# Batched matmul: stores of batches 28 to 30 through SP's queue, x loaded four batches ahead, transposes beside their own matmuls

## The chip, the cores and the metric

One core of a Trainium2 chip; the experiments ran on three chips, each time beside the kernel before. The metric is device time in microseconds (us). Where the text gives a moment ("at 496.45 us"), it is counted from the start of the profiled span, which is shorter than the device time of the same run. A landing is the issue of a transfer plus its time to landing; the views print the latter to 0.1 us, the hundredths are from the trace itself. One run was profiled for each kernel, so a moment comes from one run and a time from several.

## The reference

```python
def setup_inputs():
    batch, m, k, n = 32, 512, 1024, 768
    return {"x": randn(batch, m, k) as float32, "weight": randn(batch, k, n) as float32}

def reference(x, weight):
    return np.matmul(x, weight).astype(np.float32)
```

In float32 a batch is 2.10 MB of x, 3.15 MB of weight ("w" below) and 1.57 MB of output. All 32 batches are 167.77 MB read and 50.33 MB written, and nothing can be reused between batches.

## The kernel before

Loads go through GpSimd's queue (the "software queue") and are converted to bf16 on the way. x is transposed by TensorE against an identity matrix; the products are gathered in PSUM, copied to SBUF and stored. Batches 28 to 31 load w in pieces (`CHUNKED`), so that matmuls can begin on the first piece.

```python
    CHUNKED = {B - 4: (4, 4), B - 3: (4, 4), B - 2: (4, 4), B - 1: (4, 2, 2)}
    AHEAD = 3
    # ... w_pool bufs=4, x_pool bufs=4, xT_pool bufs=8, out_pool bufs=7 ...

    def load_x(b):      # GpSimd's queue, float32 in HBM -> bf16 in SBUF
        xs[b] = x_pool.tile([P, MT, K], BF16, name="x_sb")
        nc.gpsimd.dma_start(out=xs[b], in_=x_view[b])
    # ... load_w: the same, in the pieces of CHUNKED ...

        for b in range(1, AHEAD):
            load_x(b)
            load_w(b)
        ready = {}
        for b in range(B):
            if b + AHEAD < B:
                load_x(b + AHEAD)
                load_w(b + AHEAD)
            if b > 0:
                nc.gpsimd.dma_start(out=out_view[b - 1], in_=outs[b - 1])
            outs[b] = out_pool.tile([P, MT * N], F32, name="out_sb")
            # ... batches not in CHUNKED: transposes and matmuls, then `continue` ...
            xT = ready.pop(b, None) or {mt: transpose(b, mt) for mt in range(MT)}
            # ...
            for n in CHUNKED[b]:
                last = at + n == KT
                for mt in range(MT):
                    if last and b + 1 < B:      # the NEXT batch's transposes
                        ready.setdefault(b + 1, {})[mt] = transpose(b + 1, mt)
                    matmuls(pms[mt // 2], mt % 2, xT[mt], b, range(at, at + n), True)
                    # ... evacuate; the last batch is stored in two halves on SP's queue ...
```

Each engine has a program of its own. In PE's program of the last four batches, the last matmuls of a batch stand behind the transposes of the next one, which need the next x. The timeline below shows that they do wait there.

Of the kernel before, what the change touches and what calls it, by code (L numbers as in the profile page):

```python
# [1 line left out]

# [5 lines left out]

F32 = mybir.dt.float32
BF16 = mybir.dt.bfloat16  # L10


@with_exitstack
def kernel(
    ctx: ExitStack,
    tc: tile.TileContext,
    x: bass.AP,
    weight: bass.AP,
    out: bass.AP,
):  # L20
    nc = tc.nc
    B, M, K = x.shape
    _, _, N = weight.shape
    P = 128
    MT = M // P
    KT = K // P
    JT = KT // 2
    N2 = 2 * N
    CHUNKED = {B - 4: (4, 4), B - 3: (4, 4), B - 2: (4, 4), B - 1: (4, 2, 2)}
    AHEAD = 3  # L30

    const = ctx.enter_context(tc.tile_pool(name="const", bufs=1))
    first_pool = ctx.enter_context(tc.tile_pool(name="first", bufs=1))
    w_pool = ctx.enter_context(tc.tile_pool(name="w", bufs=4))
    x_pool = ctx.enter_context(tc.tile_pool(name="x", bufs=4))
    xT_pool = ctx.enter_context(tc.tile_pool(name="xT", bufs=8))
    out_pool = ctx.enter_context(tc.tile_pool(name="out", bufs=7))
    tpsum = ctx.enter_context(tc.tile_pool(name="tpsum", bufs=2, space=bass.MemoryType.PSUM))
    mpsum = ctx.enter_context(tc.tile_pool(name="mpsum", bufs=2, space=bass.MemoryType.PSUM))



    w_view = weight.rearrange("b (ki ko) n -> b ki ko n", ki=P)
    x_view = x.rearrange("b (mi mo) k -> b mi mo k", mi=P)
    out_view = out.rearrange("b (mi mo) n -> b mi (mo n)", mi=P)

    xs, ws, outs = {}, {}, {}

    def banks():
        return [mpsum.tile([P, 512], F32, name=f"pm{i}") for i in range(3)]  # L50

    def load_x(b):
        xs[b] = x_pool.tile([P, MT, K], BF16, name="x_sb")
        nc.gpsimd.dma_start(out=xs[b], in_=x_view[b])  # L54

    def load_w(b):
        ws[b] = w_pool.tile([P, KT, N], BF16, name="w_sb")
        at = 0
        for n in CHUNKED.get(b, (KT,)):
            nc.gpsimd.dma_start(out=ws[b][:, at:at + n, :], in_=w_view[b, :, at:at + n, :])  # L60
            at += n

    def transpose(b, mt):

        pt = tpsum.tile([P, JT, P], F32, name="pt")
        pairs = xs[b].bitcast(F32)
        for j in range(JT):
            nc.tensor.transpose(pt[:, j, :], pairs[:, mt, j::JT], ident)  # L68
        xT = xT_pool.tile([P, JT, P, 2], BF16, name="xT")
        nc.vector.tensor_copy(  # L70
            xT.rearrange("p j m r -> p (j m r)"), pt.bitcast(BF16).rearrange("p j m -> p (j m)")
        )
        return xT

    def transpose_first(mt):

        xT = xT_pool.tile([P, JT, P, 2], BF16, name="xT")
        for h in range(2):
            pt = tpsum.tile([P, JT, P], F32, name="pt")
            for i in range(JT):  # L80
                nc.tensor.transpose(pt[:, i, :], x_first[:, mt, JT * h + i::KT], ident)  # L81
            nc.vector.tensor_copy(  # L82
                xT[:, 2 * h:2 * h + 2].rearrange("p j m r -> p j r m"),
                pt.rearrange("p (j r) m -> p j r m", r=2),
            )
        return xT



    SPLITS = (  # L90
        ((0, 0, 0, 512), (1, 0, 512, N - 512)),
        ((1, N - 512, 0, 1024 - N), (2, 0, 1024 - N, N2 - 1024)),
    )

    def matmuls(pm, half, xT, b, kos, together):
        for ko in kos:
            for i, (bank, at, off, size) in enumerate(SPLITS[half]):
                shares = half == 1 and i == 0
                nc.tensor.matmul(  # L99
                    pm[bank][:, at:at + size],  # L100
                    xT[:, ko // 2, :, ko % 2],
                    ws[b][:, ko, off:off + size],
                    start=(ko == 0 and not (together and shares)),
                    stop=(ko == KT - 1),
                    skip_group_check=together,
                )

    def evacuate(b, pair, pm):
        o = outs[b][:, pair * N2:(pair + 1) * N2]
        nc.scalar.copy(o[:, 0:512], pm[0])  # L110
        nc.vector.tensor_copy(o[:, 512:1024], pm[1])  # L111
        nc.scalar.copy(o[:, 1024:N2], pm[2])  # L112

    with tc.manual_schedule():
        x_first = first_pool.tile([P, MT, K], F32)
        nc.sync.dma_start(x_first, x_view[0])
        load_w(0)
        ident = const.tile([P, P], F32)
        make_identity(nc, ident)
        for b in range(1, AHEAD):  # L120
            load_x(b)
            load_w(b)

        ready = {}
        for b in range(B):
            if b + AHEAD < B:
                load_x(b + AHEAD)
                load_w(b + AHEAD)
            if b > 0:
                nc.gpsimd.dma_start(out=out_view[b - 1], in_=outs[b - 1])  # L130
            outs[b] = out_pool.tile([P, MT * N], F32, name="out_sb")
            if b not in CHUNKED:
                turn = transpose if b else lambda _, mt: transpose_first(mt)
                xT = {mt: turn(b, mt) for mt in (0, 1)}
                for pair in range(2):
                    pm = banks()
                    for half in range(2):
                        if pair == 0:
                            matmuls(pm, half, xT[half], b, range(KT), False)
                            xT[2 + half] = turn(b, 2 + half)  # L140
                        else:
                            matmuls(pm, half, xT[2 + half], b, range(KT), False)
                    evacuate(b, pair, pm)
                continue
            xT = ready.pop(b, None) or {mt: transpose(b, mt) for mt in range(MT)}
            pms = [banks() for _ in range(2)]
            at = 0
            for n in CHUNKED[b]:
                last = at + n == KT
                for mt in range(MT):  # L150
                    if last and b + 1 < B:
                        ready.setdefault(b + 1, {})[mt] = transpose(b + 1, mt)
                    matmuls(pms[mt // 2], mt % 2, xT[mt], b, range(at, at + n), True)
                    if last and mt % 2 == 1:
                        pair = mt // 2
                        evacuate(b, pair, pms[pair])
                        if b == B - 1:
                            cols = slice(pair * N2, (pair + 1) * N2)
                            nc.sync.dma_start(out_view[b, :, cols], outs[b][:, cols])
                at += n  # L160


# [1 line left out]
_INS = ['x', 'weight']  # L164
_OUTS = [((32, 512, 768), 'float32')]


# [23 lines left out]
```

## Time and profile before

| | before |
|---|---|
| device time, median of the first 3 runs | 516.96 us (516.54 to 517.15) |
| profiled span | 516.0 us |
| software queue's packets, share of 16 engines' span | 98.9% |
| TensorE (PE) busy | 83% |
| last piece of w lands | 496.45 us |
| last matmul ends | 508.5 us |
| last store lands | 514.8 us |

These are lines of the page of the kernel before. The DMA row gives the busy share of the 16 DMA engines in tenths, in 40 slices of the span (9 means 90% or more); the queue lines give packets, bytes on the SBUF side, and the share of 16 engines' time.

```profile
span 516.0 us, 5924 instructions
PE 426.4 (83%) x2528; PEld 279.6 (54%) x2576; DVE 129.7 (25%) x196; ACT 76.3 (15%) x129; POOL 53.4 (10%) x105
...
DMA  8999999999999999999999999999999999999996
...
q0 software_dynamic: 14256, 131.60, 98.9%
q1 hardware_dynamic: 432, 3.67, 1.9%
...
HBM read 167.77 MB, written 50.33 MB: 423 GB/s over the span
...
DMA 88%; PE 9%; issue 1%; DVE 0%; ACT 0%; POOLq 0%
```

The DMA engines are busy for 90% or more of each slice from the second to the last but one.

The tail needs a closer look. This is the timeline of PE before: start, duration, instruction, count, and in brackets how long PE had been idle and what ended that.

```profile
479.18 6.66 PE L99 MATMUL pm<-w_sb,xT 128*128 128x256 bf16 x39
489.12 0.75 PE L68 MATMUL pt<-ident,x_sb 128*128 128x128 f32 x4 [3.28 <-DMA x_sb<-in_x_dram]
```

Line 68 is the transpose of batch 31. PE idled 3.28 us for x of batch 31 while batch 30's last matmuls stood behind it, although the last w of batch 30 had landed at 480.55. This is the wait that the change aims at.

Now the same tail by stretches of time. The last two numbers of a line are the share of the DMA engines that was busy and GB/s.

```profile
core 0: us, PE busy (x) PEld busy (x) DVE busy (x) ACT busy (x) POOL busy (x), PEclk, DMA share, GB/s
496.00:506.00 10.00, 9.95 (x64) 6.16 (x63) 1.38 (x2) 1.17 (x2) 0.53 (x1) 1.00 0.99 420
506.00:509.00 3.00, 2.54 (x16) 1.36 (x14) 1.33 (x2) 2.14 (x4) 0.00 (x0) 1.00 0.50 211
509.00:511.00 2.00, 0.00 (x0) 0.00 (x0) 0.05 (x1) 0.16 (x1) 0.00 (x0) 1.00 1.01 415
511.00:513.00 2.00, 0.00 (x0) 0.00 (x0) 0.00 (x0) 0.00 (x0) 0.00 (x0) 1.00 0.80 326
```

From 506 to 509 us half of the engines' time is unused, and yet the stores go on landing about 3.66 us apart (503.80, 507.45, 511.11). We read this as: each transfer is spread over the engines and has landed when the slowest part is through; some engines have run empty by then, others never do. The records carry no engine number, so this reading is inferred.

These are the last piece of w (issued at 468.65) and the last store (issued at 509.18); the last number is the time from issue to landing:

```profile
w_sb<-in_weight_dram POOLq DMA_DIRECT2D x1, 384.0 KB, 27.8
out_dram<-out_sb SPq DMA_DIRECT2D x1, 768.0 KB, 5.6
```

### The profile page before, as it was taken

How to read it: one execution, taken by the hardware profiler on the slowest of the kernel's cores; microseconds unless marked ns; L12 is line 12 of the kernel's file. 1: busy time of each engine (PE TensorE's matmuls, PEld its weight loads, DVE VectorE, ACT ScalarE, POOL GpSimd, SP SyncE). 2: the span in 40 equal slices, each digit the busy share in tenths (PEclk: the TensorE clock that was granted, in tenths of full speed). 3: DMA queues.
4: the chain of work that ended last, by engine and by line, in shares of the span. 5: the costliest groups of instructions: out<-in, count | busy, mean ns of one | idle time of the engine just before them, and what ended most of it. 6: DMA issues, size and time to landing. Idle time of an engine off the chain costs nothing.

```text
span 516.0 us, 5924 instructions
## 1 busy us (share of the span) xinstructions
PE 426.4 (83%) x2528; PEld 279.6 (54%) x2576; DVE 129.7 (25%) x196; ACT 76.3 (15%) x129; POOL 53.4 (10%) x105
## 2 busy tenths in 40 slices
PE   0999998698887879977798797987878987969794
PEld 0766665465554555654555464654545554646462
DVE  0433333133131231322313232222223132312221
ACT  0111111011111111110111011111111110101111
POOL 3011010100101001100011001010100110111000
PEclk9999999799898997998989799898989898979989
DMA  8999999999999999999999999999999999999996
GB/s 255 218 218 211 215 274 275 272 272 241 255 280 273 275 254 241 276 277 274 267 240 268 274 276 272 247 252 278 275 274 256 247 267 275 276 267 239 259 390 261
DMA packets 14714, 135.65 MB, mean 263 GB/s; under 512 B 1632, under 2 KB 1632, under 8 KB 3040
## 3 DMA queue, kind: packets, MB, share of 16 engines
q0 software_dynamic: 14256, 131.60, 98.9%
q1 hardware_dynamic: 432, 3.67, 1.9%
q8 instruction: 20, 0.33, 0.2%
q14 instruction: 6, 0.05, 0.0%
HBM read 167.77 MB, written 50.33 MB: 423 GB/s over the span
## 4 chain that ended last, share of the span: by engine, by line
DMA 88%; PE 9%; issue 1%; DVE 0%; ACT 0%; POOLq 0%
DMA x_sb<-in_x_dram 37%; DMA w_sb<-in_weight_dram 25%; DMA out_dram<-out_sb 24%; PE pm L99 7%; DMA x_first<-in_x_dram 2%; PE pt L81 1%; PE pt L68 1%; DVE out_sb L111 0%; DVE xT L70 0%; ACT out_sb L112 0%; POOLq L130 0%; POOLq L54 0%; POOLq L60 0%
## 5 line engine op out<-in xcount | busy, mean ns | idle before, releaser
L99 PE MATMUL pm<-w_sb,xT 128*128 128x256 bf16 (+1 forms) x2000 | 370.2, 340 | 60.9 <-DMA w_sb<-in_weight_dram 56.8
L99 PEld LDWEIGHTS <-xT 128*128 128x128 bf16 x2048 | 206.8, 102 | 198.3 <-issue 66.5
L70 DVE COPY xT<-pt 128x1024 bf16<-128x1024 bf16 x124 | 83.0, 689 | 245.4 <-PE pt L68 245.4
L68 PE MATMUL pt<-ident,x_sb 128*128 128x128 f32 x496 | 77.4, 290 | 8.9 <-DMA x_sb<-in_x_dram 8.6
L68 PEld LDWEIGHTS pt<-ident,x_sb 128*128 128x128 f32 x496 | 73.7, 207 | 17.2 <-issue 7.1
L110 ACT COPY out_sb<-pm 128x512 f32<-128x512 f32 x64 | 37.5, 586 | 289.6 <-PE pm L99 280.7
L111 DVE COPY out_sb<-pm 128x512 f32<-128x512 f32 x64 | 43.9, 687 | 115.5 <-PE pm L99 114.8
L112 ACT COPY out_sb<-pm 128x512 f32<-128x512 f32 x64 | 37.5, 586 | 142.5 <-PE pm L99 142.4
L54 POOL DMA_DIRECT2D x_sb<-in_x_dram x31 | 16.5, 533 | 172.8 <-DMA w_sb<-in_weight_dram 141.6
L60 POOL DMA_DIRECT2D w_sb<-in_weight_dram x37 | 19.8, 534 | 132.4 <-DMA out_dram<-out_sb 65.6
L130 POOL DMA_DIRECT2D out_dram<-out_sb x31 | 16.6, 536 | 140.8 <-DMA x_sb<-in_x_dram 62.8
L81 PE MATMUL pt<-ident,x_first 128*128 128x128 f32 x32 | 5.7, 338 | 12.4 <-DMA x_first<-in_x_dram 12.4
L81 PEld LDWEIGHTS pt<-ident,x_first 128*128 128x128 f32 x32 | 4.9, 202 | 13.0 <-issue 12.3
L82 DVE CAST xT<-pt 128x512 bf16<-128x512 f32 x8 | 5.5, 727 | 18.4 <-PE pt L81 18.3
L110 ACT ACT_TABLE_LOAD x1 | 1.3, 1283 | 0.7 <-PEq L175 0.7
masks.py:199 POOL TENSOR_SCALAR_AFFINE_SELECT ident<-ident 128x128 f32<-128x128 f32 x1 | 0.3, 288 | 0.1
masks.py:197 POOL MEMSET ident<- 128x128 f32 x1 | 0.2, 223 | 0.0
L175 POOL MEMSET const-float32-0.0<- 128x1 f32 x1 | 0.1, 99 | 0.2 <-issue 0.2
L175 POOL MEMSET const-bfloat16-1.0<- 128x1 bf16 x1 | 0.1, 102 | 0.0
L175 POOL MEMSET const-uint8-127<- 128x1 uint8 x1 | 0.1, 102 | 0.0
L175 POOL MEMSET const-float32-1.0<- 128x1 f32 x1 | 0.1, 98 | 0.0
## 6 DMA issues: line engine op xcount, KB each, us to landing
out_dram<-out_sb POOLq DMA_DIRECT2D x31, 1536.0 KB, 41.9
w_sb<-in_weight_dram POOLq DMA_DIRECT2D x28, 1536.0 KB, 43.2
x_sb<-in_x_dram POOLq DMA_DIRECT2D x31, 1024.0 KB, 39.6
w_sb<-in_weight_dram POOLq DMA_DIRECT2D x7, 768.0 KB, 32.5
x_first<-in_x_dram SPq DMA_DIRECT2D x1, 2048.0 KB, 11.5
out_dram<-out_sb SPq DMA_DIRECT2D x2, 768.0 KB, 5.3
w_sb<-in_weight_dram POOLq DMA_DIRECT2D x2, 384.0 KB, 28.7
```

Source lines behind the costliest of these rows:

```text
L54: nc.gpsimd.dma_start(out=xs[b], in_=x_view[b])
L60: nc.gpsimd.dma_start(out=ws[b][:, at:at + n, :], in_=w_view[b, :, at:at + n, :])
L68: nc.tensor.transpose(pt[:, j, :], pairs[:, mt, j::JT], ident)
L70: nc.vector.tensor_copy(xT.rearrange("p j m r -> p (j m r)"), pt.bitcast(BF16).rearrange("p j m -> p (j m)"))
L81: nc.tensor.transpose(pt[:, i, :], x_first[:, mt, JT * h + i::KT], ident)
L82: nc.vector.tensor_copy(xT[:, 2 * h:2 * h + 2].rearrange("p j m r -> p j r m"), pt.rearrange("p (j r) m -> p j r m", r=2),)
L99: nc.tensor.matmul(pm[bank][:, at:at + size], xT[:, ko // 2, :, ko % 2], ws[b][:, ko, off:off + size], start=(ko == 0 and not (together an ...
L110: nc.scalar.copy(o[:, 0:512], pm[0])
L111: nc.vector.tensor_copy(o[:, 512:1024], pm[1])
L112: nc.scalar.copy(o[:, 1024:N2], pm[2])
L130: nc.gpsimd.dma_start(out=out_view[b - 1], in_=outs[b - 1])
L175: nc = _bacc.Bacc("TRN2", target_bir_lowering=False, num_devices=1)
```

## The change

The intent: get batch 30 out of the wait for x of batch 31, by putting transposes beside the matmuls that use them and by loading x earlier; and keep stores from standing before the last loads, by sending those of batches 28 to 30 through SP's queue. SP's program waits for batch 30 first. That wait is the gate: no late store is issued before it opens (495.14 us in the changed kernel; run 3, with batch 28 first, issued its first at 464.58).

```diff
+    LATE = 4
-    x_pool = ctx.enter_context(tc.tile_pool(name="x", bufs=4))
+    x_pool = ctx.enter_context(tc.tile_pool(name="x", bufs=5))
@@ start
+        load_x(AHEAD)
-        ready = {}
         for b in range(B):
+            if b + AHEAD + 1 < B:
+                load_x(b + AHEAD + 1)
             if b + AHEAD < B:
-                load_x(b + AHEAD)
                 load_w(b + AHEAD)
-            if b > 0:
+            if 0 < b <= B - LATE:
                 nc.gpsimd.dma_start(out=out_view[b - 1], in_=outs[b - 1])
+            if b == B - 1:
+                for late in (B - 2, *range(B - LATE, B - 2)):
+                    nc.sync.dma_start(out_view[late], outs[late])
@@ the last four batches
-            xT = ready.pop(b, None) or {mt: transpose(b, mt) for mt in range(MT)}
+            xT = {0: transpose(b, 0)}
@@
-                    if last and b + 1 < B:
-                        ready.setdefault(b + 1, {})[mt] = transpose(b + 1, mt)
+                    if mt + 1 not in xT and mt + 1 < MT:
+                        xT[mt + 1] = transpose(b, mt + 1)
```

## The prediction

> **What bounds the kernel now.** The DMA engines, almost throughout. The page's queue table has the software queue at 98.9% of 16 engines' span; the 40 slices show DMA at 9 from the second to the last but one; the chain of waits is 88% DMA. PE is busy 83% and only follows. Issue times (timeline) plus times to landing show transfers landing in issue order without a hole: in the steady part w takes 7.28 us, x 4.85, a store 3.67, so 15.80 us a batch. A 3.15 MB w in 7.28 us is 432 GB/s. The Trainium skill, "DMA: Bandwidth & Descriptors", section "Where 436 GB/s comes from", puts the ceiling of the ports at 435 GB/s; this trace agrees. 32 batches at 15.80 us are 505.6 us (estimate from those landings); the rest of the 516.0 us span is about 3.6 us of start, about 5 us of single transfers landing 0.5 to 1.1 us late, and 1.2 us after the last landing.
>
> **The tail before.** x of batch 31 lands at 489.1 us, and batch 31's transposes stand in PE's program ahead of batch 30's last matmuls; PE idles 3.28 us for it (timeline). The last piece of w lands at 496.45 us, the last matmul ends only at 508.5. Yet DMA isn't waiting for that: stores of batches 27 to 30 land at 500.1, 503.8, 507.45 and 511.1, and the two halves of batch 31 at 513.0 and 514.8, 1.83 us apart, the full rate again. Some engines run dry at about 506 to 509 us; those that finish last never do.
>
> **What the change does.** It removes no byte. It moves x one batch earlier; moves three stores (3 x 3.67 = 11 us) from the software queue behind the gate on batch 30 in SP's queue; and lets batch 30's matmuls run without x of batch 31. The stores up to batch 26 precede the last w in both kernels, so the last w is still due at about 496.5 us. Batch 30 should be done at 491 to 492 us instead of 499; SP issues then, its 11 us of stores share the engines with the last w pieces and the store of batch 27, and the last w may slip to about 500. PE then ends at 502 to 506 us instead of 508.5, but the same 18 us of stores remain for DMA. The skill (same page, section "Issuing engines are not separate DMA queues") says that transfers from both queues run on the same 16 engines and interleave; I expect no added bandwidth. So nearly all of the gain on PE lies off the critical path.
>
> **Predicted time:** 516.5 us, 8 times in 10 between 514.5 and 518.5. Faster by over 2%: 0.01; within 2%: 0.97; slower by over 2%: 0.02.
>
> **What would show each step.** Right: the same bytes, a steady batch of 15.80 us, PE's 3.28 us wait for x of batch 31 gone, last matmul 3 to 6 us earlier, yet the last landing within 1.5 us of 514.8. Wrong: slices of the tail below 9 (a hole between the gate and the software queue's end), a longer start, or two queues together moving clearly over 432 GB/s.
>
> **What would make it wrong.** If the engine that lands last is late because of the software queue itself, fewer software stores give back up to about 3 us. If the early late landings (some 2 us of w between 60 and 107 us) vanish because x is further ahead, the same. If SP's stores starve the last w so long that batch 31 comes after the other stores are through, DMA idles and it loses a few us.

## More of the kernel before

The profiled run of the kernel before took 517.73 us, 0.8 us over its median; that of the changed kernel 517.39. So moments of two traces are best compared from a common event, such as the landing of the last w.

## The result, and the profile after

| | before | after |
|---|---|---|
| device time, median (range), 6 runs each | 516.94 us (516.54 to 518.18) | 517.33 us (517.03 to 518.65) |
| last piece of w lands | 496.45 us | 495.91 us |
| last matmul ends | 508.5 us | 507.3 us |
| last store lands | 514.80 us | 514.26 us |

The ratio after to before is 1.0008, 95% interval 0.9993 to 1.0022: the same. A ratio here is the mean time of one kernel's runs over that of the other kernel's runs of the same rounds, so it is not quite the ratio of the medians quoted. All runs below lie within 2% of before; what is read of them are differences clear of the interval. Where an experiment is compared with the changed kernel below, the two ratios to the kernel before are divided, or the medians subtracted, as the text says; these come from different rounds.

The page of the changed kernel:

```profile
span 515.6 us, 5976 instructions
PE 429.0 (83%) x2576; PEld 279.2 (54%) x2576; DVE 129.8 (25%) x196; ACT 76.3 (15%) x129; POOL 51.9 (10%) x102
...
DMA  8999999999999999999999999999999999999996
...
q0 software_dynamic: 13824, 126.88, 96.8%
q1 hardware_dynamic: 864, 8.39, 4.0%
...
HBM read 167.77 MB, written 50.33 MB: 423 GB/s over the span
...
DMA 89%; PE 7%; issue 1%; POOL 1%; DVE 0%; ACT 0%; POOLq 0%
```

The three late stores moved from the software to the hardware queue: 98.9 to 96.8% and 1.9 to 4.0%. The sum, the bytes and the 40 digits of DMA are the same.

The timeline of PE after:

```profile
481.35 2.26 PE L100 MATMUL pm<-w_sb,xT 128*128 128x512 bf16 x8 [3.38 <-DMA w_sb<-in_weight_dram]
...
495.74 1.48 PE L100 MATMUL pm<-w_sb,xT 128*128 128x512 bf16 x8 [0.30 <-DVE xT L71]
...
499.31 7.96 PE L100 MATMUL pm<-w_sb,xT 128*128 128x512 bf16 x48
```

The wait for x is gone. In its place PE waits 3.38 us for the first piece of w of batch 30, which landed at 481.21 us, where it was 476.89 us before: x of batch 31 now stands ahead of it in the same queue. The wait was turned into another one. From there PE needs about 13 us for each of the last two batches and ends at 507.3, only 1.3 us earlier. Some 1.6 of these 26 us come from a drop of the granted clock in this one execution (0.72 on average from 481 to 487 us): run 5 had 1.00 there and went from its first piece of w to PE's end in 24.4 us instead of 26.1.

The stretches of the tail after, columns as above:

```profile
494.00:496.00 2.00, 1.70 (x13) 1.35 (x12) 1.69 (x3) 0.59 (x1) 0.00 (x0) 1.00 0.72 286
496.00:506.00 10.00, 10.00 (x65) 6.48 (x64) 1.82 (x4) 0.59 (x1) 0.00 (x0) 1.00 1.01 426
506.00:509.00 3.00, 1.27 (x8) 0.59 (x6) 1.23 (x2) 1.71 (x3) 0.00 (x0) 1.00 0.92 387
509.00:511.00 2.00, 0.00 (x0) 0.00 (x0) 0.00 (x0) 0.00 (x0) 0.00 (x0) 1.00 0.97 402
511.00:513.00 2.00, 0.00 (x0) 0.00 (x0) 0.00 (x0) 0.00 (x0) 0.00 (x0) 0.89 0.35 144
```

The dry spell moved from 506 to 509 us to the moment before the gate opens (SP issues its stores at 495.14 us; run 3, with batch 28 first, issued its first at 464.58). After 511 us an engine share of 0.35, or 5.6 of 16 engines' worth, is left working for the last landing. The last piece of w (issued at 469.32) and the last store (issued at 507.92):

```profile
w_sb<-in_weight_dram POOLq DMA_DIRECT2D x1, 384.0 KB, 26.6
out_dram<-out_sb SPq DMA_DIRECT2D x1, 768.0 KB, 6.3
```

Both kernels need exactly as long from the last w to the last store: 514.80 - 496.45 = 18.35 us before, 514.26 - 495.91 = 18.35 us after. Five stores' worth of transfers (batches 27 to 31) at 3.67 us each is 18.35 us. So there was no hole in what finishes last in either kernel; that the dry spells were those of engines with time to spare follows from the sum, not from a view of single engines. The 0.54 us by which the last store lands earlier after was there at the last w already.

### The profile page after: what moved, and what is told of

The parts are those of the page before. It is cut to its first block, busy times and chain, and to the rows that moved or that the text cites. A ratio compares the mean times of both kernels' runs of the same rounds, so it can differ in the third digit from the quotient of the medians. Undisturbed runs are those within 1.5% of the kernel's fastest.

```text
span 515.6 us, 5976 instructions
## 1 busy us (share of the span) xinstructions
PE 429.0 (83%) x2576; PEld 279.2 (54%) x2576; DVE 129.8 (25%) x196; ACT 76.3 (15%) x129; POOL 51.9 (10%) x102
## 3 DMA queue, kind: packets, MB, share of 16 engines
q0 software_dynamic: 13824, 126.88, 96.8%
## 4 chain that ended last, share of the span: by engine, by line
DMA 89%; PE 7%; issue 1%; POOL 1%; DVE 0%; ACT 0%; POOLq 0%
DMA w_sb<-in_weight_dram 39%; DMA x_sb<-in_x_dram 25%; DMA out_dram<-out_sb 25%; PE pm L100 7%; PE pt L69 1%; POOL w_sb L61 0%; POOL x_sb L55 0%; ACT out_sb L113 0%; DVE out_sb L112 0%; DVE xT L71 0%; POOL ident masks.py:199 0%; POOL ident masks.py:197 0%; POOLq L132 0%; POOLq L61 0%; POOLq masks.py:199 0%
## 5 line engine op out<-in xcount | busy, mean ns | idle before, releaser
L100 PE MATMUL pm<-w_sb,xT 128*128 128x256 bf16 (+1 forms) x2048 | 374.1, 342 | 66.1 <-DMA w_sb<-in_weight_dram 63.7
L69 PE MATMUL pt<-ident,x_sb 128*128 128x128 f32 x496 | 75.3, 285 | 0.0
L132 POOL DMA_DIRECT2D out_dram<-out_sb x28 | 15.1, 538 | 119.0 <-DMA x_sb<-in_x_dram 57.3
L82 PE MATMUL pt<-ident,x_first 128*128 128x128 f32 x32 | 6.0, 350 | 12.2 <-DMA x_first<-in_x_dram 12.2
L82 PEld LDWEIGHTS pt<-ident,x_first 128*128 128x128 f32 x32 | 5.0, 204 | 12.8 <-issue 12.2
```

The source lines that it names most:

```text
L69: nc.tensor.transpose(pt[:, j, :], pairs[:, mt, j::JT], ident)
L82: nc.tensor.transpose(pt[:, i, :], x_first[:, mt, JT * h + i::KT], ident)
L100: nc.tensor.matmul(pm[bank][:, at:at + size], xT[:, ko // 2, :, ko % 2], ws[b][:, ko, off:off + size], start=(ko == 0 and not (together an ...
```

## The experiments

Theory A: the engine that lands last never waits in the tail, so only its bytes count. Rivals: parts of the change cancel each other (B); the gate or the late stores matter by themselves (C). Theory D came up after the first four runs.

| run | median, us | ratio to before of the same rounds (95%) |
|---|---|---|
| transposes alone | 518.28 | 1.0023 (1.0008 to 1.0038) |
| late stores alone | 517.18 | 1.0013 (0.9992 to 1.0034) |
| no gate | 522.58 | 1.0106 (1.0090 to 1.0123) |
| half of the matmuls (wrong result) | 516.07 | 0.9980 (0.9965 to 0.9995) |
| two late stores left out (wrong result) | 512.86 | 0.9927 (0.9911 to 0.9943) |
| two middle stores left out (wrong result) | 509.57 | 0.9853 (0.9840 to 0.9867) |
| transposes, two late stores | 518.49 | 1.0025 (1.0013 to 1.0038) |
| last store by GpSimd | 520.84 | 1.0072 (1.0058 to 1.0085) |
| x three ahead | 517.24 | 1.0009 (0.9996 to 1.0021) |
| no late stores | 517.72 | 1.0013 (0.9997 to 1.0029) |
| all stores on SP | 522.18 | 1.0101 (1.0088 to 1.0114) |

### 1. The transposes alone

The kernel before with the last two hunks of the change's diff only.

> The kernel before with one part of the change alone: in the last four batches each transpose stands with its own batch's matmuls. Theory A (the DMA engine that lands last never waits in the tail, so only its queued bytes count): batch 30's matmuls no longer wait for x of batch 31, the 3.28 us wait of PE there is gone and the last matmul ends 3 us or more before 508.5 us; the last landing stays within 1 us of 514.8 and the time within 0.3% of before. Rival B (parts of the change cancel: the transposes gain and the late stores lose): 2 us or more faster than before.

Measured: the last matmul ended at 505.0 us, 3.5 us earlier than before. The last store landed at 513.80, 1.0 us earlier, but that isn't a gain of the transposes: the last w too landed 1.0 us earlier (495.41), and at 107 us, where the two kernels don't differ yet, an x landed 1.3 us earlier (106.25 and 107.58). It is a difference between two executions. From the last w to the last store it was 18.39 us, as before. The ratio is 1.0023: not faster, if anything 1 us slower. Rival B is out for this part. The missing microsecond has a visible place. The program's end on GpSimd is a DRAIN instruction. This is its line (duration min/median/max in ns, first and last start), first in the kernel before, then in this run:

```profile
L186 POOLq DRAIN  x3: 46/102/16031, 499.2 to 515.7; - x3
```

```profile
L185 POOLq DRAIN  x3: 46/93/25479, 489.9 to 515.8; - x3
```

And these are the last transfers of the software queue, issued at 499.19 and at 489.88 us (the last number is the time from issue to landing), again before and this run:

```profile
out_dram<-out_sb POOLq DMA_DIRECT2D x1, 1536.0 KB, 11.9
```

```profile
out_dram<-out_sb POOLq DMA_DIRECT2D x1, 1536.0 KB, 21.4
```

Before, the drain ran from 499.2 for 16.03 us, to 515.2; the last software transfer had landed at 511.1. Here it ran from 489.9 for 25.48 us, to 515.3, with the landing at 511.3. In both it ended 4.1 us after the last landing of the software queue. Before, SP was through at 514.9, so the drain came 0.3 us later; here SP was through at 513.9 and the drain came 1.4 us later. That is theory D. Counted from the last w, the last software landing came after 14.66 us before and 15.84 us here: PE was done sooner, so SP issued its first store at 504.4 and not at 507.9, and its transfers ran beside the software queue's last store. So the drain ended 1.2 us later from the last w (19.93 against 18.75 us). That is as much as this run's times lie above before's (0.0023 of 517 is 1.2 us); the two profiled runs, 517.87 and 517.73 us, don't show it because of the 1.0 us that this one was ahead. It rests on one trace of each kernel.

### 2. The late stores alone

The kernel before with `LATE = 4` and the two hunks of the stores; x three ahead, transposes as before.

> The kernel before with the late stores alone: stores of batches 28 to 30 on SP's queue behind the gate on batch 30, x three ahead and the transposes as before. The gate opens at about 499 us, when the software queue has about 1 us left. Theory A: the engines that run ahead stand dry for some us before 500, the one that lands last for at most 1 us, so 0 to 1.5 us slower than before. Rival B: 2 us or more slower. If a dry spell of the faster engines costs time by itself, over 3 us slower.

Measured: 1.0013, the interval from 0.4 us faster to 1.8 us slower. The gate opened at 497.0 us. This is the stretch just before:

```profile
494.00:498.00 4.00, 4.00 (x28) 2.69 (x27) 1.40 (x3) 1.17 (x2) 0.00 (x0) 1.00 0.57 232
```

The engines were busy 0.57 of 4 us, so 1.7 us of a mean engine's time lay idle, and the last store still landed at 513.33, or 18.35 us after the last w (494.98): the same 18.35 as in the other two. This dry spell cost nothing. Theory A holds, B (2 us or more slower) doesn't.

### 3. No gate

The changed kernel with one line changed:

```diff
-                for late in (B - 2, *range(B - LATE, B - 2)):
+                for late in range(B - LATE, B - 1):
```

> The changed kernel with the three late stores in the order 28, 29, 30, so that nothing holds back the first two. They are issued at about 465 and 480 us and share the engines with the last loads. Theory A: the last w lands up to 7 us later than 495.9, the last matmul ends up to 4 us later than 507.3, but the bytes are the same and the time is 0 to 2 us over the changed kernel's. Rival C (the gate protects the last w, and the kernel needs it): 4 us or more slower.

Measured: 1.0106, some 5 us slower than the changed kernel by both ways of comparing. Rival C was right and my bound of 2 us was wrong. Of this run, first a line of PE's timeline, then the stretches of the tail:

```profile
487.78 2.72 PE L100 MATMUL pm<-w_sb,xT 128*128 128x512 bf16 x8 [10.12 <-DMA w_sb<-in_weight_dram]
```

```profile
507.00:510.00 3.00, 3.00 (x21) 1.84 (x19) 0.69 (x1) 0.00 (x0) 0.00 (x0) 1.00 0.23 98
510.00:515.00 5.00, 4.95 (x31) 2.76 (x29) 0.92 (x2) 1.73 (x4) 0.00 (x0) 1.00 0.00 0
```

The early stores took turns with the last loads, so PE waited 10.12 us for w of batch 30 and finished at 514.9. By then every other transfer was through, and the DMA engines, all 16 of them, stood at 0.00 for 5 us. Theory A isn't contradicted in its core (a hole in the last engine costs its full length), but it had only counted bytes. The order of the transfers decides whether PE is ready with the last store in time.

### 4. Half of the matmuls in batches 0 to 27 (wrong result)

```diff
+            few = (0, 1, 2, KT - 1)
-  matmuls(..., b, range(KT), False)      # both calls in batches not in CHUNKED
+  matmuls(..., b, few, False)
```

> The changed kernel with half of the matmuls of batches 0 to 27 left out (wrong result on purpose); the tail and all transfers are unchanged. PE busy falls from 429 to about 290 us. If PE's work were on the critical path, many us faster. Theory A: only what the instruction fetches cost is saved. 1792 fewer PE instructions should leave about 13 of the 20 fetches of 16 KB in the instruction queue; in both traces three landings of the last engine came 1.1 us late just after a fetch, so one or two of these should vanish: 0 to 2.5 us faster. If fetches don't matter: within 0.5 us.

Measured: PE busy fell from 429 to 310 us (the granted clock was 0.82 here and 0.94 in the changed kernel); the time was 1.0 us under before's by the ratio and 1.3 us under the changed kernel's by the medians. Two lines of this run's page, PE and the instruction queue:

```profile
PE 310.0 (60%) x1680; PEld 205.4 (40%) x1680; DVE 129.9 (25%) x196; ACT 76.3 (15%) x129; POOL 51.9 (10%) x102
...
q8 instruction: 13, 0.21, 0.1%
```

PE's work outside the tail is off the critical path: 119 us less of it gave 1.3 us. From the last w to the last store it was 18.38 us, so the gain came before the tail: the last w landed at 494.70, 1.2 us earlier than in the changed kernel. That this is due to the 7 fetches of 16 KB fewer (20 before, 13 here) fits the expectation, but the records carry no engine number, and executions of unlike kernels differed by as much at the last w (496.45 before, 495.41 in run 1), so it is argued and not shown.

### 5 and 6. The same bytes taken out in the tail and in the middle (wrong results on purpose)

```diff
# 5: batches 28 and 29 are never stored
-                for late in (B - 2, *range(B - LATE, B - 2)):
+                for late in (B - 2,):
# 6: batches 10 and 11 are never stored
-            if 0 < b <= B - LATE:
+            if 0 < b <= B - LATE and b - 1 not in (10, 11):
```

> The changed kernel without two of its late stores (batches 28 and 29 are never written: wrong result on purpose). 7.3 us of transfers less, right in the tail. If transfers alone bound the tail: 7.3 us faster than the changed kernel. Theory A': PE is close behind there (last matmul at 507.3 us), so DMA now waits for PE; the last store is issued at about 508 us and lands some 3.8 us later, as in the run without a gate: about 512, only 2 to 3 us faster.

> The changed kernel without the stores of batches 10 and 11 (never written: wrong result on purpose): the same 3.15 MB as in the run without two late stores, taken out in the middle. Theory A: everything after them comes 7.3 us earlier and the time is 6.5 to 8 us under the changed kernel's. If transfers weren't the bound in the middle: under 3 us.

Measured, by medians against the changed kernel's 517.33: 7.8 us saved in the middle, 4.5 us in the tail (8.0 and 4.2 by the ratios). Two stores are 7.3 us of transfers. In the middle a byte is worth its full time, as theory A says. In the tail part of it turned into a hole, as two stretches of run 5 show:

```profile
502.00:505.00 3.00, 2.95 (x19) 1.66 (x17) 0.69 (x1) 1.66 (x3) 0.00 (x0) 1.00 0.00 0
505.00:509.00 4.00, 0.19 (x1) 0.00 (x0) 0.69 (x1) 0.64 (x2) 0.00 (x0) 1.00 0.93 381
```

From 502 to 505 us nothing was transferred; PE's end (505.2) released the last store, which landed 3.85 us after its issue. From the last w to the last store it was 14.23 us, where the three stores left are worth 11.0: a hole of 3.2 us. 7.3 less 3.2 is 4.1 us, close to the saving measured. The saving was above the 2 to 3 us expected because PE ended at 505.2 and not at 507.3: its first groups of 8 matmuls in batch 30 took 1.46 us each and not 2.26 and 1.97, at a granted clock of 1.00 and not 0.72 (481 to 487 us).

### 7. The transposes with two late stores, x three ahead

The run with the transposes alone, plus `LATE = 3` and `for late in (B - 2, B - 3)` on SP.

> The kernel before with the transposes beside their own matmuls, and the stores of batches 30 and 29 on SP's queue, gated by batch 30; x stays three ahead. In the traces so far GpSimd's drain at the program's end ended 4.0 to 4.1 us after the last landing of the software queue: in the run with the transposes alone this came 1.4 us after SP was done. Here the last software landing should be 3 us or more earlier, so the drain is hidden. Theory D (the drain cost what the transposes gained): 0.5 to 2 us faster than the run with the transposes alone, and 0 to 1.2 us faster than before. Rival: no difference from the run with the transposes alone.

Measured: 1.0025, no different from the transposes alone. As a way to hide the drain this was a miss: SP's two stores were issued at 490 us and took turns with what stood in the software queue, so the last software landing came later (512.2 us), not earlier. GpSimd's drain in this run:

```profile
L189 POOLq DRAIN  x3: 46/159/39563, 476.6 to 517.0; - x3
```

The drain ran 39.56 us from 476.6, to 516.2: 4.0 us after that landing and 2.1 us after SP's last store landed (514.03). So the forecast was wrong and the trace still fits theory D.

### 8. The last store by GpSimd

```diff
-  nc.sync.dma_start(out_view[b, :, cols], outs[b][:, cols])
+  queue = nc.sync if pair == 0 else nc.gpsimd
+  queue.dma_start(out_view[b, :, cols], outs[b][:, cols])
```

> The changed kernel with its very last store (the second half of batch 31) issued by GpSimd instead of SP: the same bytes at the same moment. Theory D: the drain ends about 4 us after that landing and so ends the program: 3 to 4.5 us slower than the changed kernel. If the drain costs nothing at the end: within 1 us.

Measured: 1.0072, which is 3.3 us over the changed kernel by the ratios and 3.5 by the medians, as expected. Its last store even landed a bit earlier than the changed kernel's. Of this run: the issue of that store in GpSimd's timeline, its time to landing, and the drain:

```profile
508.61 0.54 POOL L165 DMA_DIRECT2D out_dram<-out_sb  x1 [35.41 <-ACT out_sb L113]
```

```profile
out_dram<-out_sb POOLq DMA_DIRECT2D x1, 768.0 KB, 4.9
```

```profile
L192 POOLq DRAIN  x3: 46/241/8900, 508.6 to 518.4; - x3
```

It landed at 508.6 + 4.9 = 513.5 us (514.26 in the changed kernel), and the drain ended at 508.6 + 8.9 = 517.5, so 4.0 us later. This shows the cost by itself: who issues the very last store is worth 3.3 us.

### 9 and 10. One part of the change taken back

Run 9 has `AHEAD = 3` for x again with `bufs=4`; run 10 has the stores of batches 28 to 30 back on GpSimd's queue.

> The changed kernel with x three batches ahead as before (late stores and transposes stay). Batch 30's first half of w should land some 4 us earlier (about 477 instead of 481 us), so PE ends at 503 to 506 us instead of 507.3, the gate opens at about 490 instead of 495 and the late stores share the engines with the last w. Theory A (bytes and the engine that lands last decide; with all late stores on SP the drain of the software queue ends before 512 us and is hidden): within 0.3% of the changed kernel, last landing 513.3 to 514.8. Rival (x four ahead matters, for or against): more than 0.4% apart.

> The changed kernel with the stores of batches 28 to 30 back in the software queue (x four ahead and transposes stay). Theory A with D: the last software landing comes at about 510.7 us, GpSimd's drain ends 4 us after it, at about 514.8, and the program about 0.75 us after that or after SP, whichever is later: 0 to 1 us slower than the changed kernel. Rival (the late stores are what costs in the changed kernel): 1 us or more faster than it.

Measured: 1.0009 and 1.0013 against 1.0008 for the whole change; neither can be told from it. In run 9 PE ended at 503.7 us, 3.6 us earlier than in the changed kernel, because w of batch 30 no longer stood behind x of batch 31, and the last store landed at 514.16, 0.1 us earlier. So loading x four ahead costs PE its gain, and PE's gain is worth nothing. Here the late stores did take turns with the last pieces of w (499.48), and it cost nothing: one store's worth of transfers was done before the last w, and from there the last store took 14.68 us, four stores' worth at 3.67. PE was ready in time. In run 10 the last software landing was 510.9 us and the drain ended at 515.0, 0.8 us after SP was through: small enough to drown in the spread of the runs.

### 11. All stores on SP

```diff
-                nc.gpsimd.dma_start(out=out_view[b - 1], in_=outs[b - 1])
+                nc.sync.dma_start(out=out_view[b - 1], in_=outs[b - 1])
```

> The changed kernel with the stores of batches 0 to 27 on SP's queue too. Tests the clause of the prediction that the software queue itself makes the last engine late: then 1 to 3 us faster than the changed kernel. Theory A: no gain from the queue; SP's stores no longer stand behind some 42 us of loads, so stores of batches 26 and 27 come before the last w, which lands 3 to 7 us later than 495.9, and PE with it; DMA then runs dry for a moment before the last store: 0 to 4 us slower than the changed kernel.

Measured: 1.0101, about 5 us slower than the changed kernel, above the 4 us that I had allowed. The two queues on this run's page, and the stretches around its gate:

```profile
q0 software_dynamic: 9792, 82.84, 75.7%
q1 hardware_dynamic: 4896, 52.43, 24.4%
```

```profile
497.00:501.00 4.00, 4.00 (x26) 2.44 (x25) 0.69 (x1) 1.37 (x3) 0.00 (x0) 1.00 0.33 66
501.00:504.00 3.00, 2.64 (x18) 1.93 (x18) 1.97 (x3) 0.97 (x2) 0.00 (x0) 1.00 0.16 66
504.00:515.00 11.00, 10.90 (x68) 6.89 (x68) 2.30 (x4) 1.72 (x4) 0.00 (x0) 1.00 0.98 411
```

A quarter of the transfers' time now ran on SP's queue, and nothing was won by it. The stores no longer stood behind the loads, so the last w came at 500.9 us, the software queue ran empty, and the engines had little to do until the gate opened at 502.8. A store itself is as fast on either queue: SP's late stores landed 3.65 us apart in the changed kernel, the software queue's last ones 3.67 before.

No kernel beats the one before.

## Why the prediction was right

The time (516.5 predicted, 517.33 measured, range 514.5 to 518.5) and the verdict were right. As the range also holds "no change at all", the number alone says little; what counts is the mechanism. Point by point:

- **The bound.** Right. The same bytes at the same 423 GB/s over the span, and the same steady batch. Runs 4 and 6 show it causally: 119 us less of PE's work gave 1.3 us, 7.3 us fewer transfers in the middle gave 7.8.
- **The gain lies off the critical path.** Right. Three arrangements of the tail (before, after, late stores alone) have 18.35 us from the last w to the last store, with PE ending at three different times. Run 9 moved PE's end by another 3.6 us for 0.1 us of landing.
- **PE ends at 502 to 506 us.** Wrong in size: it ended at 507.3, and the gate opened at 495.1 instead of 491 to 492. The mis-sized term is the start of batch 30. I kept w of batch 30 where it had been and forgot that the moved x stands before it in the same queue: its first piece came at 481.21 instead of 476.89, and PE then needed some 26 us for the two batches. Run 9 takes that part away and gives 503.7. A last matmul 3 to 6 us earlier was one of my signs of being right; it failed, without harm to the time because PE's end was off the critical path. The drop of the granted clock (1.6 us, above) added to the miss by chance.
- **The last w may slip to about 500.** It didn't (495.91), because the gate opened so late. Where the gate opened at 490 (run 9) it slipped to 499.5.
- **A hole before the gate as a sign of error.** The hole was there (share 0.72 from 494 to 496 us) and cost nothing. I had named the wrong sign: what counts is whether the engines that finish last have a hole, as in run 3, where all stood still for 5 us.
- **"If SP's stores starve the last w".** Shown by runs 3 and 11: about 5 us slower, even more than the "few us" that I had given it.
- **"If the engine that lands last is late because of the software queue itself".** Run 11 gives it no support (the order of the transfers changed there too, so it doesn't refute it either). But the software queue has a cost at the end that the prediction didn't contain: the drain, 4 us after its last landing. Before, it outlasted SP by 0.3 us; the change hid it.

What stays open: why the engines don't finish together, why the last w lands up to 1.5 us apart in kernels that are the same until batch 28 (496.45 before, 494.98 in run 2), and whether the 0.4 us of the changed kernel over before is anything; its interval includes no difference at all.

## What to carry to other kernels

Where one resource is full from start to end, count what a change takes from that resource; here reordering gained nothing, as it only moved holes that were free, and twice it lost 5 us. In the tail such a kernel has two limits close together, and the order of transfers decides whether the last store finds its data ready: what can wait may take turns with the last loads only as far as PE is still ready in time (run 9 lost nothing by it, run 3 5 us). Look at what follows the last landing of a queue: here GpSimd's drain ended some 4 us after its last store, SP's drains took 7 ns each, and the last store on SP's queue was 3.3 us better than on GpSimd's.

## What the Trainium skill lacked or had wrong

- "VectorE: DVE Perf Modes", section "The DRAIN you can't avoid", describes the drains of a program's start and end as about 12 ns, constant, on all engines. GpSimd's drain at the end lasted 16.0 us before and 25.5 us in run 1, and ended 3.9 to 4.1 us after the last landing of the software queue in all twelve traces where that transfer was a store (2.8 us in run 11, where it was a load of w). The trace puts it on the line of the program's `TileContext`, so it may not be one of the drains that the page means; then the page isn't wrong but lacks this one. No page that I looked at names this cost; run 8 shows it worth 3.3 us.
- "DMA: Bandwidth & Descriptors", section "Where 436 GB/s comes from", says that for HBM to SBUF transfers the limit of HBM per core, about 358 GB/s, binds. With one core at work this trace had 423 GB/s over the whole span, loads and stores together, and 432 GB/s for a load of w. The sentence lacks its condition: the same page, section "Bandwidth", has 358 GB/s for two cores streaming and 425 GB/s for one, which this trace agrees with. What no page that I looked at has is how a transfer that converts is to be counted: the 432 GB/s are float32 bytes read; as bf16 only 216 GB/s arrived in SBUF, so a load of w doesn't show the limit of the SBUF ports (435 GB/s) that the prediction names.
- The same page, section "Issuing engines are not separate DMA queues", says that the issuing engine saves only issue time. The bandwidth agrees (run 11), but that section leaves out that the queue also decides order (section "Queues, rings and completion order" has each engine take turns between the queues): a store on SP overtakes loads that stand in GpSimd's queue (in run 11 one landed 12.2 us after its issue, with some 40 us of loads queued), which cost 5 us in runs 3 and 11.
